# First chunk of tile 0's normalised rows: ScalarE writes the high part from the bank, VectorE the values beside it

## The chip, the core and the metric

The kernel runs on one core of one Trainium2 chip. The metric is the device time of one execution in microseconds (us). Three runs of the kernel before gave 1754.39, 1754.5 and 1756.76 us; their median is 1754.5 us.

The engines are named as the profile names them: PE (TensorE) multiplies, and its weight loads are PEld; DVE is VectorE, ACT ScalarE, POOL GpSimd; SP issues the loads from memory. Each works through its own list of instructions in order.

## The reference

One decoder layer on 256 rows of 2048 values in float32: a half-step SwiGLU FFN, then attention (eight MLA heads and eight NSA heads that read one combined input projection), then a second half-step FFN. After each of the three a DeepNorm layer norm:

```
x = layer_norm(ALPHA * x + 0.5 * swiglu(x, ffn1...), ln1_g, ln1_b)
mix = concat(mla(x @ w_in), nsa(x @ w_in)) @ w_out
x = layer_norm(ALPHA * x + mix, ln2_g, ln2_b)
x = layer_norm(ALPHA * x + 0.5 * swiglu(x, ffn2...), ln3_g, ln3_b)
```

## The kernel before

**Numbers in two parts.** PE reads operands in a rounded 32-bit format. To keep float32 accuracy each operand is held as a high part (the rounded value) and a low part (what the rounding left). `split` (L94 to L96) makes them: ACT casts the value to the high part, DVE subtracts the high part from the value. Weights become `whi` and `wlo`, activations `thi` and `tlo`. `mm3` (L98 to L102) makes one product of three matmuls, always in the order thi by whi (L100), thi by wlo (L101), tlo by whi (L102). PE takes them in that order, so the third one waits for `tlo` with all that follows.

**Stages.** FFN 1, input projection and attention, output projection, FFN 2. The 256 rows are two tiles of 128 rows (t = 0, 1). A row of 2048 values has four chunks of 512, n = 0 to 3. Weights stream from memory in pieces of 128 x 1024 (tiles `raw`, or `sum` from a second pool), which ACT and DVE split before PE uses them. So ACT and DVE serve two masters: the weight pieces, and everything that is done to activations.

**The layer norm in between.** When the last chunk of a tile's rows is complete, `ln` (L597) starts for that tile. DVE and ACT bring the rows to mean 0 and variance 1 (L594 to L608). Then `norm_T` (L567) goes chunk by chunk: PE turns the chunk's four 128 x 128 blocks round into one PSUM bank (L575). DVE takes blocks 0 and 2 out of the bank, multiplied by the gain and with the bias added (L584), ACT does the same for blocks 1 and 3 (L582), into a work tile `w`. At last `split` makes `thi` by an ACT cast of 128 x 512 (L95) and `tlo` by a DVE subtraction (L96). `w` is returned, since after the second layer norm sums of its blocks are needed too (L405 to L408).

`ln` runs this twice with consequences for the next stage: after FFN 1 (called ln1) for the input projection, and after attention (ln2) for FFN 2. In both, tile 0 goes first, while PE still finishes tile 1 of the stage before, and the next stage begins with products of chunk 0 of tile 0. Its first weight pieces are ready long before (they lie in tiles `m`).

**Who sets the order.** PE and SP take their instructions as the code issues them. ACT, DVE and POOL are put in order by a scheduler that plays the program through with times of its own, and gives the instruction of the highest priority that it holds ready; `tc.high_priority()` lifts what is written under it. Once built, the order is fixed. L384 and L1045 are DVE's additions of a finished bank to the residual rows `y` and L565 its statistics of them; they stand between the others in the lists below.

Of the kernel before, what the change touches and what calls it, by code (L numbers as in the profile page):

```python
# [13 lines left out]
AF = mybir.ActivationFunctionType  # L14
OP = mybir.AluOpType
# [38 lines left out]
def layer(ctx: ExitStack, tc: tile.TileContext, a: dict, out: bass.AP):  # L54
    nc = tc.nc
    PE, V, A, G = nc.tensor, nc.vector, nc.scalar, nc.gpsimd
# [12 lines left out]
    f = lambda t: t.bitcast(F32)  # L69
# [14 lines left out]
    def wk(shape):  # L84
        w = work.tile([P, NCH], F32, name="w", bufs=NW)
        if len(shape) == 3:
            return w[:, :shape[1] * shape[2]].rearrange("p (a b) -> p a b", a=shape[1])
        return w
# [5 lines left out]
    def split(hi, lo, src):  # L94
        A.copy(hi, src)  # L95
        V.tensor_tensor(lo, src, f(hi), op=OP.subtract)  # L96
# [87 lines left out]
    def new_bank():  # L184
        return bank.tile([P, NCH], F32, name="bank")
# [202 lines left out]
    def new_T():  # L388
        return (tp.tile([P, 4, P], F32R, name="thi"), tp.tile([P, 4, P], F32R, name="tlo"))
# [174 lines left out]
            st[t] = stat.tile([P, 4, 6], F32, name=f"bn{t}", bufs=1)  # L564
        V.bn_stats(st[t][:, n, :], y[t][:, n * NCH:(n + 1) * NCH])  # L565

    def norm_T(src, gcol, bcol, dst, k0):  # L567

        pt = new_bank().rearrange("p (a b) -> p a b", a=4)
        nj = src.shape[1] // P
        for j in range(nj):
            PE.transpose(pt[:, j, :], src[:, j * P:(j + 1) * P], ident)  # L575
        v = wk([P, 4, P])
        for j in range(nj):
            k = k0 + j
            if bcol is None:
                V.tensor_scalar(v[:, j, :], pt[:, j, :], gcol[:, k:k + 1], None, op0=OP.mult)  # L580
            elif j % 2:
                A.activation(v[:, j, :], pt[:, j, :], AF.Identity, bias=bcol[:, k:k + 1], scale=gcol[:, k:k + 1])  # L582
            else:
                V.tensor_scalar(v[:, j, :], pt[:, j, :], gcol[:, k:k + 1], bcol[:, k:k + 1], op0=OP.mult, op1=OP.add)  # L584
        if isinstance(dst, tuple):
            dst = [dst]
        step = nj // len(dst)
        for i, (hi, lo) in enumerate(dst):
            split(hi[:, :step, :], lo[:, :step, :], v[:, i * step:(i + 1) * step, :])
        return v  # L590

    def ln_rows(t, eps):
        mv = stat.tile([P, 2], F32, name="mv")
        V.bn_aggr(mv, st[t].rearrange("p a b -> p (a b)"))  # L594
        return mv[:, 0:1], rstd_of(mv[:, 1:2], eps)

    def ln(t, name, eps, x, xs=None):  # L597

        yc = [y[t][:, n * NCH:(n + 1) * NCH] for n in range(4)]
        with tc.high_priority():  # L600
            mu, r = ln_rows(t, eps)
            mr = stat.tile([P, 1], F32, name="mr")
            V.scalar_tensor_tensor(mr, mu, -1.0, r, op0=OP.mult, op1=OP.mult)
            for n in range(4):
                if n % 2 == 0:
                    V.tensor_scalar(yc[n], yc[n], mu, r, op0=OP.subtract, op1=OP.mult)
                else:
                    A.activation(yc[n], yc[n], AF.Identity, bias=mr, scale=r)  # L608
        yield DLN
        for n in range(4):  # L610
            x[n, t] = new_T()
            v = norm_T(yc[n], cst[name + "_g"], cst[name + "_b"], x[n, t], 4 * n)
            for j in range(2):
                if xs is not None and 2 * n + j in UP7:
                    xs.setdefault(2 * n + j, []).extend(v[:, 2 * j + i, :] for i in range(2))
            yield 1
# [20 lines left out]
    cst = {}  # L637
# [15 lines left out]
    def done1(t, n):  # L653
        ln_stats(t, n)
        if n == 3:
            spawn(ln(t, "ln1", 4 * LN_EPS, x1))
            steps()
# [49 lines left out]
    def fin_a(t, ps):  # L707
        def go():
            o = rms(ps, QR)
            yield DTR  # L710
            norm_T(o, cst["mla_q_norm_g"], None, lat(cq, t, 2), 0)

        spawn(go())
        steps()

    def fin_b(t, ps):
        def go():
            o = rms(ps[:, :KVR], KVR)
            kr = wk([P, 2, P])
            V.memset(kr, 0.0)  # L720
            rope(kr[:, 0:1, :RD], ps[:, KVR:KVR + RD].rearrange("p (h d) -> p h d", h=1), cst["cos64"][:, t, :],
                 cst["sin64"][:, t, :], 1, RD)
            V.tensor_copy(kr[:, 1, RD:], kr[:, 0, :RD])
            z = stat.tile([P, 24], F32, name="gz")
            V.tensor_tensor(z, ps[:, KVR + RD:KVR + RD + 24], cst["nsa_gate_b"], op=OP.add)
            A.activation(z, z, AF.Exp, scale=-1.0)
            V.tensor_scalar(z, z, 1.0, None, op0=OP.add)
            V.reciprocal(gates[:, t, :], z)
            yield DTR + 2
            norm_T(o, cst["mla_kv_norm_g"], None, lat(ckv, t, 1), 0)  # L730
            pt = new_bank().rearrange("p (a b) -> p a b", a=4)
            for j in range(2):
                PE.transpose(pt[:, j, :], kr[:, j, :], ident)
            A.copy(krT[:, :, t, :], pt[:, 0:2, :])

        spawn(go())
        steps()
# [315 lines left out]
    def out_last(ks, ns):  # L1053

        held = {}
        for t in range(NT):
            for n in ns:
                ps = new_bank()
                if t == 0:
                    held[n] = [(ks[i:i + KT], load(W["w_out"], n, ks[i:i + KT])) for i in range(0, len(ks), KT)]  # L1060
                for pc, wp in held[n]:
                    for k, (hi, lo) in zip(pc, wp):
                        mm3(ps, mixer(k, t), hi, lo, k == ks[0], k == ks[-1])
                    tick(1)
                out_fin(t, ps, n, False)
                ln_stats(t, n)
            spawn(ln(t, "ln2", LN_EPS, x2, xs2))
            steps()
# [123 lines left out]
```

## Time and profile before

| | |
|---|---|
| three runs | 1754.39, 1754.5, 1756.76 us, median 1754.5 us |
| the profiled execution | 1758.64 us, its span 1756.9 us |
| PE busy | 1736.7 us (99%) |
| DVE busy | 1586.5 us (90%) |
| ACT busy | 1023.5 us (58%) |
| granted TensorE clock, mean of the span | 0.997 |

The profile is of one execution, which took 4.1 us more than the median of the three runs; 1.7 us of its time lie outside the span. Times in a timeline are us from the start of the span. A row of it gives start, duration, engine, line, operation, what is written and read, how many instructions are merged in the row and, in square brackets, how long the engine had been idle and what ended that. Matmuls overlap, so what one of them costs is read from start to start (0.23 us for 128 x 512 at full clock), not from its duration; for ACT and DVE too the distance from start to start is a little shorter than the duration.

### The profile page before, as it was taken

What the parts mean: (1) busy time and instruction counts of PE and PEld (TensorE: products, weight loads), DVE (VectorE), ACT (ScalarE), POOL (GpSimd) and SP (SyncE); (2) the same over time, 40 slices, a digit from 0 to 9 for tenths busy, and PEclk for the clock granted to TensorE, in tenths of its full rate; (3) what the DMA queues carried; (4) which work ended last, traced back from release to release, by engine and by line L of the source; (5) the groups of instructions that cost most, each with busy time, mean ns of one, the idle gap of its engine ahead of it and who ended that gap; (6) DMA issues with size and microseconds to landing.
All of it is one profiled execution on the core that took longest, in us unless ns stands there. A gap on an engine that the chain in (4) does not pass through costs nothing. (4 is left out here: it accounts for less than half of the span.)

```text
span 1756.9 us, 22430 instructions
## 1 busy us (share of the span) xinstructions
PE 1736.7 (99%) x8040; PEld 1428.9 (81%) x8040; DVE 1586.5 (90%) x2099; ACT 1023.5 (58%) x1354; POOL 17.0 (1%) x39
## 2 busy tenths in 40 slices
PE   9999999999999999999999999999999999999997
PEld 7888888888888887887788788888888888888886
DVE  7899999999999998865586679899999999999998
ACT  6656565565656665654365545665655565656652
POOL 0000000000000000000000001000000000000000
PEclk9999999999999999999999999999999999999999
DMA  9665656556666566546753345654656655665665
GB/s 337 218 216 172 212 198 215 185 188 200 212 206 220 168 203 232 178 159 213 260 193 131 120 169 175 216 196 168 215 192 215 205 195 200 206 201 192 204 203 180
DMA packets 100336, 350.01 MB, mean 199 GB/s; under 512 B 11136, under 2 KB 13696, under 8 KB 100224
## 3 DMA queue, kind: packets, MB, share of 16 engines
q1 hardware_dynamic: 98944, 344.39, 58.4%
q0 software_dynamic: 1280, 4.20, 0.9%
q8 instruction: 63, 1.03, 0.2%
q14 instruction: 49, 0.40, 0.1%
HBM read 346.44 MB, written 2.10 MB: 198 GB/s over the span
## 5 line engine op out<-in xcount | busy, mean ns | idle before, releaser
L100 PE MATMUL bank<-whi,thi 128*128 128x512 f32 (+1 forms) x1904 | 748.6, 393 | 1.5 <-ACT whi L95 1.5
L101 PE MATMUL bank<-wlo,thi 128*128 128x512 f32 (+1 forms) x1904 | 740.8, 389 | 3.2 <-DVE wlo L96 3.1
L102 PE MATMUL bank<-whi,tlo 128*128 128x512 f32 (+1 forms) x1904 | 740.0, 389 | 0.2 <-DVE tlo L96 0.2
L95 ACT CAST whi<-raw 128x1024 fp32r<-128x1024 f32 (+1 forms) x577 | 540.6, 962 | 270.5 <-PE bank L102 142.9
L96 DVE TENSOR_TENSOR wlo<-raw,whi 128x1024 fp32r<-128x1024 f32 (+1 forms) x577 | 631.6, 1109 | 61.0 <-ACT whi L95 60.1
L95 ACT CAST whi<-sum 128x1024 fp32r<-128x1024 f32 x271 | 282.5, 1050 | 337.8 <-DVE sum L328 124.3
L100 PEld LDWEIGHTS bank<-whi,thi 128*128 128x128 f32 x1904 | 357.9, 188 | 79.3 <-issue 4.1
L101 PEld LDWEIGHTS bank<-wlo,thi 128*128 128x128 f32 x1904 | 358.1, 188 | 77.5 <-DVE wlo L96 7.0
L102 PEld LDWEIGHTS bank<-whi,tlo 128*128 128x128 f32 x1904 | 357.8, 188 | 74.3 <-DVE tlo L96 0.6
L96 DVE TENSOR_TENSOR wlo<-sum,whi 128x1024 fp32r<-128x1024 f32 x271 | 324.9, 1216 | 32.4 <-ACT whi L95 29.9
L100 PE MATMUL bank<-whi,m 128*128 128x512 f32 x448 | 174.3, 389 | 0.0
L101 PE MATMUL bank<-wlo,m 128*128 128x512 f32 x448 | 174.3, 389 | 0.0
L102 PE MATMUL bank<-whi,m 128*128 128x512 f32 x448 | 174.3, 389 | 0.0
L326 DVE TENSOR_TENSOR sum<-raw 128x1024 f32<-128x1024 f32 x112 | 136.7, 1220 | 12.4 <-DMA raw<-in_ffn_w_up 10.5
L101 PEld LDWEIGHTS bank<-wlo,m 128*128 128x128 f32 x448 | 84.1, 188 | 17.5
L102 PEld LDWEIGHTS bank<-whi,m 128*128 128x128 f32 x448 | 84.1, 188 | 17.5
L100 PEld LDWEIGHTS bank<-whi,m 128*128 128x128 f32 x448 | 84.1, 188 | 17.5
L328 DVE TENSOR_TENSOR sum<-sum,raw 128x512 f32<-128x512 f32 x112 | 76.9, 686 | 0.2
L327 DVE TENSOR_TENSOR sum<-sum,raw 128x512 f32<-128x512 f32 x112 | 76.8, 686 | 0.1
L384 DVE TENSOR_TENSOR w<-bank,w 128x512 f32<-128x512 f32 x80 | 51.8, 683 | 2.2 <-PE bank L102 2.2
L777 ACT ACTIVATE w<-w,mx 128x256 f32<-128x256 f32 (+1 forms) x48 | 21.3, 445 | 27.5 <-DVE mx L773 24.6
L384 DVE TENSOR_TENSOR y<-bank,w 128x512 f32<-128x512 f32 x32 | 20.7, 683 | 6.8 <-PE bank L102 6.8
(187 smaller groups left out, 946.5 us busy)
## 6 DMA issues: line engine op xcount, KB each, us to landing
raw<-in_ffn_w_down SPq DMA_DIRECT2D x176, 512.0 KB, 4.5
raw<-in_ffn_w_up SPq DMA_DIRECT2D x160, 512.0 KB, 4.7
raw<-in_ffn_w_gate SPq DMA_DIRECT2D x146, 512.0 KB, 4.7
raw<-in_ffn_gu SPq DMA_DIRECT2D x32, 512.0 KB, 5.0
raw<-in_w_in SPq DMA_DIRECT2D x30, 512.0 KB, 5.2
raw<-in_w_out SPq DMA_DIRECT2D x20, 512.0 KB, 3.3
sum<-in_w_in SPq DMA_DIRECT2D x18, 512.0 KB, 5.3
sum<-in_ffn_w_gate SPq DMA_DIRECT2D x12, 512.0 KB, 4.8
```

The costliest lines, as they stand in the source:

```text
L95: A.copy(hi, src)
L96: V.tensor_tensor(lo, src, f(hi), op=OP.subtract)
L100: PE.matmul(ps, xh, wh, start=first and not onto, stop=False, skip_group_check=onto)
L101: PE.matmul(ps, xh, wl, start=False, stop=False, skip_group_check=onto)
L102: PE.matmul(ps, xl, wh, start=False, stop=last, skip_group_check=onto)
L326: V.tensor_tensor(t13, a_, b_[:, 1:2, :].broadcast_to([P, 2, NCH]), op=OP.add)
L327: V.tensor_tensor(t24[:, 0], t13[:, 0], a_[:, 1], op=OP.add)
L328: V.tensor_tensor(t24[:, 1], t24[:, 0], b_[:, 0], op=OP.add)
L384: V.tensor_tensor(r, B[b], rest[b], op=OP.add)
L777: A.activation(s[:, h, :], s[:, h, :], AF.Exp, bias=mx[:, h:h + 1], accum_out=sm[:, h:h + 1])
```

## The change

`norm_T` gets a flag `first`, which `ln` sets for chunk 0 of tile 0 alone. It holds at both layer norms, so two of the sixteen chunks are concerned. For these, ACT writes all four blocks of `thi` straight from the bank, gain and bias applied (four instructions of 128 x 128), DVE writes the values of all four blocks into `w` beside it (four more), and DVE subtracts. The ACT cast of 128 x 512 is gone. All of it stands under `tc.high_priority()`.

```diff
-    def norm_T(src, gcol, bcol, dst, k0):
+    def norm_T(src, gcol, bcol, dst, k0, first=False):
...
         v = wk([P, 4, P])
+        if first:
+            with tc.high_priority():
+                for j in range(nj):
+                    g, b = gcol[:, k0 + j:k0 + j + 1], bcol[:, k0 + j:k0 + j + 1]
+                    A.activation(dst[0][:, j, :], pt[:, j, :], AF.Identity, bias=b, scale=g)
+                    V.tensor_scalar(v[:, j, :], pt[:, j, :], g, b, op0=OP.mult, op1=OP.add)
+                V.tensor_tensor(dst[1], v, f(dst[0]), op=OP.subtract)
+            return v
         for j in range(nj):
...
-            v = norm_T(yc[n], cst[name + "_g"], cst[name + "_b"], x[n, t], 4 * n)
+            v = norm_T(yc[n], cst[name + "_g"], cst[name + "_b"], x[n, t], 4 * n, t == 0 and n == 0)
```

In the changed kernel L581 is ACT's write of `thi`, L582 DVE's of `w`, L583 the subtraction; the lines that follow moved down by eight (DVE's L584 is L592, ACT's L582 is L590, L594 is L602, L1045 is L1053). PE, SP and POOL keep their orders. In the built program the eight instructions on the bank take turns: each L582 waits for the L581 of its block, and the next L581 for that L582.

DVE at ln1, from the first split of a weight piece after the rows were normalised to `tlo` of chunk 0 (the last row). Before, chunk 0's two and chunk 1's first two L584 and one of chunk 2 stand ahead of it:

```order
L96 TENSOR_TENSOR wlo<-raw,whi 128x1024
L584 TENSOR_SCALAR w<-bank,pack 128x128
L96 TENSOR_TENSOR wlo<-sum,whi 128x1024
L584 TENSOR_SCALAR w<-bank,pack 128x128 x2
L384 TENSOR_TENSOR y_93<-bank,w 128x512
L584 TENSOR_SCALAR w<-bank,pack 128x128
L565 BN_STATS bn_5629<-y_93 128x6
L584 TENSOR_SCALAR w<-bank,pack 128x128
L594 BN_AGGR mv<-bn_5629 128x2
L96 TENSOR_TENSOR tlo<-w,thi 128x512
```

Now, after the same `wlo<-raw`, another `wlo<-sum`, one L582 and one L592, the list goes on to `tlo` like this:

```order
L96 TENSOR_TENSOR wlo<-sum,whi 128x1024
L582 TENSOR_SCALAR w<-bank,pack 128x128
L592 TENSOR_SCALAR w<-bank,pack 128x128 x2
L582 TENSOR_SCALAR w<-bank,pack 128x128
L384 TENSOR_TENSOR y_93<-bank,w 128x512
L592 TENSOR_SCALAR w<-bank,pack 128x128
L565 BN_STATS bn_5629<-y_93 128x6
L582 TENSOR_SCALAR w<-bank,pack 128x128
L602 BN_AGGR mv<-bn_5629 128x2
L96 TENSOR_TENSOR wlo<-sum,whi 128x1024
L558 TENSOR_SCALAR rstd<-mv 128x1
L583 TENSOR_TENSOR tlo<-w,thi 128x512
```

Ahead of `tlo` of chunk 0 stand now three `wlo<-sum` instead of one, eight instructions of 128 x 128 instead of five, and `rstd` of tile 1.

ACT at the same place, from the first weight cast after the rows were normalised; before, up to the cast that makes `thi` of chunk 0:

```order
L95 CAST whi<-raw 128x1024
L95 CAST whi<-sum 128x1024 x2
L582 ACTIVATE w<-bank,pack 128x128
L95 CAST whi<-sum 128x1024
L95 CAST whi<-raw 128x1024
L582 ACTIVATE w<-bank,pack 128x128 x2
L95 CAST thi<-w 128x512
```

Now, up to the fourth block of chunk 0 (the cast of `thi` in it is chunk 1's):

```order
L95 CAST whi<-raw 128x1024
L95 CAST whi<-sum 128x1024
L581 ACTIVATE thi<-bank,pack 128x128
L95 CAST whi<-sum 128x1024 x2
L581 ACTIVATE thi<-bank,pack 128x128
L590 ACTIVATE w<-bank,pack 128x128
L95 CAST whi<-raw 128x1024
L581 ACTIVATE thi<-bank,pack 128x128
L590 ACTIVATE w<-bank,pack 128x128 x2
L95 CAST thi<-w 128x512
L581 ACTIVATE thi<-bank,pack 128x128
```

The first block comes earlier by one weight cast, but the fourth has the same five weight casts ahead of it, six small instructions instead of three, and chunk 1's cast.

DVE at ln2, from the last `wlo<-sum` before chunk 0 to `tlo` of chunk 0. Before:

```order
L96 TENSOR_TENSOR wlo<-sum,whi 128x1024
L584 TENSOR_SCALAR w<-bank,pack 128x128
L1045 TENSOR_TENSOR y_93<-bank,y_93 128x512
L584 TENSOR_SCALAR w<-bank,pack 128x128
L565 BN_STATS bn_9300<-y_93 128x6
L584 TENSOR_SCALAR w<-bank,pack 128x128
L96 TENSOR_TENSOR wlo<-raw,whi 128x1024
L96 TENSOR_TENSOR tlo<-w,thi 128x512
```

Now, after the same `wlo<-sum` and the addition to `y_93`:

```order
L582 TENSOR_SCALAR w<-bank,pack 128x128
L565 BN_STATS bn_9303<-y_93 128x6
L592 TENSOR_SCALAR w<-bank,pack 128x128
L96 TENSOR_TENSOR wlo<-raw,whi 128x1024
L582 TENSOR_SCALAR w<-bank,pack 128x128
L592 TENSOR_SCALAR w<-bank,pack 128x128 x2
L582 TENSOR_SCALAR w<-bank,pack 128x128
L1053 TENSOR_TENSOR y_93<-bank,y_93 128x512
L592 TENSOR_SCALAR w<-bank,pack 128x128
L582 TENSOR_SCALAR w<-bank,pack 128x128
L565 BN_STATS bn_9303<-y_93 128x6
L583 TENSOR_TENSOR tlo<-w,thi 128x512
```

Here `tlo` has eight instructions of 128 x 128 ahead of it instead of three, and one more addition to `y` with its statistics.

## The prediction

> **What bounds the kernel now.** I read the busy shares first, then the table of what PE waited for, then the timelines of PE, DVE and ACT round the two places of the change, and last the granted clock in stretches of 3.41 us.
>
> ```profile
> PE 1736.7 (99%) x8040; PEld 1428.9 (81%) x8040; DVE 1586.5 (90%) x2099; ACT 1023.5 (58%) x1354; POOL 17.0 (1%) x39
> PE bank L101 <- DVE wlo L96: 3.1, 6, 0.9
> PE bank L100 <- ACT thi L95: 2.2, 2, 1.8
> PE bank L100 <- ACT whi L95: 1.5, 3, 0.8
> PE bank L102 <- DVE tlo L96: 0.6, 2, 0.4
> ```
>
> PE has work for 99% of the span, so the end moves by what PE loses or gains. The rows on `thi` and `tlo` are the waits that the change can reach: 2.2 + 0.6 us in four waits. PE round ln1, and then ln2:
>
> ```profile
> 703.29 0.60 PE L575 MATMUL bank<-ident,y 128*128 128x128 f32 x4
> 705.64 0.50 PE L100 MATMUL bank<-m,thi 128*128 128x512 f32 x1 [1.75 <-ACT thi L95]
> 705.98 0.40 PE L101 MATMUL bank<-m,thi 128*128 128x512 f32 x1
> 706.37 0.50 PE L102 MATMUL bank<-m,tlo 128*128 128x512 f32 x1
> ...
> 709.01 0.40 PE L102 MATMUL bank<-m,tlo 128*128 128x512 f32 x1
> 709.32 0.51 PE L100 MATMUL bank<-whi,thi 128*128 128x512 f32 x1
> 709.66 0.39 PE L101 MATMUL bank<-wlo,thi 128*128 128x512 f32 x1
> 710.23 0.50 PE L102 MATMUL bank<-whi,tlo 128*128 128x512 f32 x1 [0.17 <-DVE tlo L96]
> 710.56 0.39 PE L100 MATMUL bank<-whi,thi 128*128 128x512 f32 x1
> ```
>
> ```profile
> 1051.24 0.60 PE L575 MATMUL bank<-ident,y 128*128 128x128 f32 x4
> 1052.33 0.50 PE L100 MATMUL bank<-m,thi 128*128 128x512 f32 x1 [0.50 <-ACT thi L95]
> 1052.67 0.40 PE L101 MATMUL bank<-m,thi 128*128 128x512 f32 x1
> 1053.48 0.50 PE L102 MATMUL bank<-m,tlo 128*128 128x512 f32 x1 [0.41 <-DVE tlo L96]
> ```
>
> Chunk 0 starts its two matmuls with `thi` (705.64, 705.98) and then needs `tlo` (706.37). Both `thi` and `tlo` are late, at ln1 by 1.75 us and a little, at ln2 by 0.50 and 0.41. Who makes them late is seen on DVE and ACT at ln1:
>
> ```profile
> 700.28 1.23 DVE L96 TENSOR_TENSOR wlo<-raw,whi 128x1024 fp32r<-128x1024 f32 x1 [0.38 <-ACT whi L95]
> 701.42 0.40 DVE L584 TENSOR_SCALAR w<-bank,pack 128x128 f32<-128x128 f32 x1
> 701.74 1.21 DVE L96 TENSOR_TENSOR wlo<-sum,whi 128x1024 fp32r<-128x1024 f32 x1
> 702.87 0.72 DVE L584 TENSOR_SCALAR w<-bank,pack 128x128 f32<-128x128 f32 x2
> 703.51 0.68 DVE L384 TENSOR_TENSOR y<-bank,w 128x512 f32<-128x512 f32 x1
> 704.11 0.40 DVE L584 TENSOR_SCALAR w<-bank,pack 128x128 f32<-128x128 f32 x1
> 704.43 0.68 DVE L565 BATCH_NORM_STATS2 bn<-y 128x6 f32<-128x512 f32 x1
> 705.12 0.41 DVE L584 TENSOR_SCALAR w<-bank,pack 128x128 f32<-128x128 f32 x1
> 705.44 0.25 DVE L594 BATCH_NORM_AGGREGATE mv<-bn 128x2 f32<-128x24 f32 x1
> 705.62 0.69 DVE L96 TENSOR_TENSOR tlo<-w,thi 128x512 fp32r<-128x512 f32 x1
> 706.23 0.15 DVE L558 TENSOR_SCALAR rstd<-mv 128x1 f32<-128x1 f32 x1
> 706.29 0.40 DVE L584 TENSOR_SCALAR w<-bank,pack 128x128 f32<-128x128 f32 x1
> ```
>
> ```profile
> 704.29 0.80 ACT L582 ACTIVATE w<-bank,pack 128x128 f32<-128x128 f32 x2
> 704.98 0.60 ACT L95 CAST thi<-w 128x512 fp32r<-128x512 f32 x1
> 705.49 0.81 ACT L582 ACTIVATE w<-bank,pack 128x128 f32<-128x128 f32 x2
> ```
>
> From 700.28 on DVE has no idle time until `tlo` is done, and ACT's rows follow each other too. Here neither engine waits for data: what counts is how much stands in the list ahead of `tlo`. PE's first matmul follows the end of the cast (704.98 + 0.60 = 705.58) by 0.06 us, its third the end of the subtraction (705.62 + 0.69 = 706.31) by 0.06 us.
>
> **The change part by part.** Each of the two chunks loses one ACT cast (0.60 us) and two L582, and gains four L581; DVE gains two instructions of 128 x 128. That work by itself is small and off the path on average (ACT is 58% busy). What counts is the order. The flag and the priority do put ACT's first block one weight cast earlier, so `thi` of block 0 is no longer what PE waits for. But `mm3` needs `tlo` as its third operand, and the one subtraction that makes it needs all four blocks.
>
> *tlo at ln1.* By the lists of DVE, up to `tlo` there are two more `wlo<-sum` (1.13 us each from start to start: 701.74 to 702.87), three more instructions of 128 x 128 (0.32 each: 701.42 to 701.74), and one `rstd` (0.06: 706.23 to 706.29). That is 2.26 + 0.96 + 0.06 = 3.28 us. ACT takes turns with DVE on the bank and holds it once: the third block has two more small ones ahead of it on ACT than the two L582 at 704.29 have (0.35 each: two of them take 704.29 to 704.98), so it ends at 704.29 + 0.70 + 0.45 = 705.44 (0.45 is one of two that take 0.80 together, 0.35 apart), while DVE would be there at 700.28 + 1.14 + 2 x 1.13 + 5 x 0.32 = 705.28. With 0.2 for this, `tlo` starts at 705.62 + 3.5 = 709.1, ends at 709.8, and the third matmul stands at 709.85 instead of 706.37: +3.5 us. ACT's fourth block is no later limit: 704.98 + 3 x 0.35 + 0.51 (the cast, 704.98 to 705.49) + 0.45 = 707.0.
>
> Some of it comes back. The four steps from 709.01 to 710.56 in the rows above take 1.55 us, of which the waits for chunk 1's parts and the restarts make 1.55 - 4 x 0.23 = 0.6. Chunk 1 is made sooner in the new lists, relative to PE, so these go. Net at ln1: +2.9 us.
>
> *tlo at ln2.* Here the list holds five more of 128 x 128 (5 x 0.32 = 1.6), one more addition to `y` (0.60, taken from 703.51 to 704.11) and its statistics (0.69, 704.43 to 705.12): 2.9 us, and with the same 0.2 for taking turns +3.1 us. PE's third matmul goes from 1053.48 to 1056.6. Behind it no wait is left to give back. Both waits hold everything behind them, since PE runs in order. SP's loads keep their order and come later by what PE is late, but so does their use.
>
> Together +6.0 us by waiting.
>
> *The clock.* The two waits are now single long ones: at ln1 from about 704.4 (transposes done at 703.89, then two matmuls) to 709.85, at ln2 from 1052.3 to 1056.6. What a gap does to the clock, in four stretches (columns: stretch, length, busy time of PE, PEld, DVE, ACT and POOL, clock, DMA, GB/s):
>
> ```profile
> 684.99:688.40 3.41, 1.73 (x6) 0.91 (x6) 1.81 (x4) 2.55 (x4) 0.00 (x0) 1.00 0.76 274
> 688.40:691.81 3.41, 3.41 (x10) 2.63 (x9) 3.08 (x6) 0.78 (x2) 0.00 (x0) 0.50 0.98 362
> 702.05:705.46 3.41, 1.84 (x11) 1.29 (x9) 3.40 (x8) 3.41 (x7) 0.00 (x0) 1.00 0.62 159
> 705.46:708.88 3.42, 3.24 (x15) 2.40 (x16) 3.07 (x9) 3.42 (x7) 0.55 (x1) 1.00 0.13 48
> ```
>
> A stretch in which PE was busy 1.73 of 3.41 us was followed by one at clock 0.50; one with 1.84 us was not. With the change 705.46 to 708.88 holds no matmul at all, so the next stretch, to 712.29, runs at half clock: PE works in it from 709.85, and loses half of 2.4, 1.2 us. At ln2, shifted by 2.9 + 1.2, the gap lies from 1056.4 to 1060.7; in steps of 3.41 the stretch 1057.04 to 1060.45 is empty, and half clock lasts to 1063.87: half of 3.2, 1.6 us. Together +2.8 us. How the gap lies to the stretches is chance in another run; moving it through one stretch, I estimate 0.9 to 2.4 us for each.
>
> The Trainium skill ("TensorE: Matmul & The Clock Gate", Part 1: The HAM clock gate) has the clock halved after an idle window of about 3.4 us, and windows that run freely. This trace is stricter: 688.40 followed a stretch that was half busy. By the page's rule a whole window must be idle, which a gap of 5.4 us need not hold and one of 4.3 seldom does; by it the clock would cost 0 to 2.8 us, and the sum would be 6.0 to 8.8.
>
> *Sum.* 6.0 + 2.8 = +8.8 us: the profiled execution's 1758.64 would be 1767.4, and the median of 1754.5, which is 4.1 lower, 1763.3 us.
>
> **The rivals.** *The priority works on the chip* (the other side). If DVE came to `tlo` no later than PE needs it, the losses at both places would go: at ln1 1.75, then 0.16 (705.98 to 706.37, less 0.23), then 0.6; at ln2 0.50 and 0.58 (1052.67 to 1053.48, less 0.23): 3.6 us, 1750.9. It decides where 3.3 us of DVE's list would vanish at ln1; DVE has no idle time there before, and the list is fixed. Chance 0.03.
>
> *Half of the shift only.* DVE's extra entries are the same weight pieces that it split right behind `tlo` before. If PE could use the work done early, a part of the wait would be paid back. Then +3, 1757.5. Against it: after 710.56 only few waits remain on PE to shorten. Chance 0.05.
>
> *No half clock, or at one place alone.* Waiting as forecast, 6.0 to 7.2 us: 1760.5 to 1761.7. For it: a stretch with 1.84 us of work kept the full clock after it. Against it: the gaps are longer than one stretch. Chance 0.2. The page's rule above is of this kind, its milder end.
>
> *Half clock for a stretch longer at each place*, if the stretch in which PE restarts doesn't count as busy: up to 1.7 us more each, half of 3.41: 1765 to 1766.7. For it: the one case in the trace was released only after a stretch with PE busy throughout (3.41). Chance 0.12.
>
> **How the numbers follow.** The forecast, waits and half clock at both places, has 0.6: 1763.3, with 1762 to 1765 as its own range. About 0.2%, 3.5 us, is what a measurement of this kernel can tell from no change. Faster by more than that (below 1751.0) is only the first rival at its full price: 0.02. Within it lie the rest of that rival and the half shift: 0.06. Slower: 0.92. The range leaves out the first two rivals (0.08) and what lies above a longer half clock: 1759.5 to 1767.0, which takes in the lowest case without half clock less 1 us for the two sums of waits.
>
> **What would show it.** In the profile of the changed kernel PE's row L102 at about 709.8 and at about 1060.7 should show the wait for `tlo` from L583, 5 and 4 us long, and L100 none for `thi`; the subtraction L583 should start near 709.1, on a DVE without idle time since 700.28 but for 0.2; the stretches behind the two gaps should have clock 0.50. Wrong would be: L583 done before 706.4, or the wait there but PE caught up by 720, or no stretch at 0.50 beside the one at 688.

## The result and the profile after

The changed kernel took 1766.09 us (median of 4 runs, 1765.72 to 1766.55) beside 1755.55 us (1754.39 to 1756.76, 4 runs: the three above and one of 1756.59) of the kernel before: ratio 1.0057, 95% interval 1.0045 to 1.0069. It is slower by 0.6%. The time lies inside the predicted range of 1759.5 to 1767.0, but 2.8 us above the predicted 1763.3 and 1.1 above the forecast's own 1762 to 1765; 1.05 of the 2.8 us are the fourth run's share in the median of before. Its profiled execution took 1765.87 us, with a span of 1764.2 us.

What PE waited for at `thi` and `tlo` is one row now (us in total, times, longest us); the row on `thi` is gone:

```profile
PE bank L102 <- DVE tlo L583: 9.6, 2, 5.3
```

PE at ln1, with the two matmuls that no longer wait and the third that does:

```profile
700.82 0.48 PE L100 MATMUL bank<-m,thi 128*128 128x512 f32 x1
701.14 0.40 PE L101 MATMUL bank<-m,thi 128*128 128x512 f32 x1
706.84 0.79 PE L102 MATMUL bank<-m,tlo 128*128 128x512 f32 x1 [5.31 <-DVE tlo L583]
707.43 0.63 PE L100 MATMUL bank<-m,thi 128*128 128x512 f32 x1
707.86 0.63 PE L101 MATMUL bank<-m,thi 128*128 128x512 f32 x1
...
710.84 0.40 PE L100 MATMUL bank<-m,thi 128*128 128x512 f32 x1
711.09 0.40 PE L101 MATMUL bank<-m,thi 128*128 128x512 f32 x1
...
712.01 0.40 PE L102 MATMUL bank<-whi,tlo 128*128 128x512 f32 x1
```

The two matmuls with `thi` run as soon as the transposes are done. The third waits 5.31 us, and the matmuls behind it come 0.43 us apart instead of 0.23, until 710.84. DVE meanwhile, from the same first weight piece as before:

```profile
697.45 1.22 DVE L96 TENSOR_TENSOR wlo<-raw,whi 128x1024 fp32r<-128x1024 f32 x1 [0.38 <-ACT whi L95]
698.60 1.22 DVE L96 TENSOR_TENSOR wlo<-sum,whi 128x1024 fp32r<-128x1024 f32 x1
699.73 0.40 DVE L582 TENSOR_SCALAR w<-bank,pack 128x128 f32<-128x128 f32 x1
...
704.49 0.40 DVE L582 TENSOR_SCALAR w<-bank,pack 128x128 f32<-128x128 f32 x1
704.80 0.25 DVE L602 BATCH_NORM_AGGREGATE mv<-bn 128x2 f32<-128x24 f32 x1
704.97 1.16 DVE L96 TENSOR_TENSOR wlo<-sum,whi 128x1024 fp32r<-128x1024 f32 x1
706.04 0.14 DVE L558 TENSOR_SCALAR rstd<-mv 128x1 f32<-128x1 f32 x1
706.10 0.68 DVE L583 TENSOR_TENSOR tlo<-w,thi 128x512 fp32r<-128x512 f32 x1
```

From the first weight piece to the start of `tlo` it is now 706.10 - 697.45 = 8.65 us; before it was 705.62 - 700.28 = 5.34. ACT's four blocks were ready before; the last one ended at 704.17, 1.93 us ahead of `tlo`:

```profile
703.69 0.48 ACT L581 ACTIVATE thi<-bank,pack 128x128 fp32r<-128x128 f32 x1
```

At ln2 the same picture, with a wait of 4.25 us:

```profile
1053.27 0.48 PE L100 MATMUL bank<-m,thi 128*128 128x512 f32 x1
1053.58 0.40 PE L101 MATMUL bank<-m,thi 128*128 128x512 f32 x1
1058.23 0.50 PE L102 MATMUL bank<-m,tlo 128*128 128x512 f32 x1 [4.25 <-DVE tlo L583]
...
1062.44 0.40 PE L102 MATMUL bank<-m,tlo 128*128 128x512 f32 x1
```

Taking turns shows there as a wait of DVE, once:

```profile
1056.58 0.41 DVE L582 TENSOR_SCALAR w<-bank,pack 128x128 f32<-128x128 f32 x1 [0.21 <-ACT thi L581]
```

The clock in stretches of 3.41 us, at ln1 (three) and at ln2 (three):

```profile
700.60:704.02 3.42, 0.93 (x7) 0.50 (x5) 3.32 (x8) 3.42 (x9) 0.00 (x0) 1.00 0.82 224
704.02:707.43 3.41, 0.59 (x1) 0.50 (x2) 2.97 (x8) 2.07 (x5) 0.93 (x1) 0.50 0.17 59
707.43:710.85 3.42, 3.42 (x12) 2.73 (x11) 3.42 (x6) 1.52 (x2) 0.00 (x0) 0.50 0.37 103
```

```profile
1052.18:1055.59 3.41, 1.80 (x10) 1.15 (x9) 3.41 (x8) 3.14 (x8) 0.00 (x0) 1.00 0.55 185
1055.59:1059.01 3.42, 0.78 (x3) 0.67 (x4) 3.21 (x9) 1.92 (x5) 0.00 (x0) 1.00 0.40 129
1059.01:1062.42 3.41, 3.41 (x11) 2.73 (x10) 2.97 (x6) 1.52 (x2) 0.86 (x1) 0.50 0.00 0
```

PE's order is the same in both kernels, so each matmul of the one can be set beside the same matmul of the other. Its start after less its start before shows where time was lost (the times of before at 691.57 and later are those of its profiled execution):

| the same instruction of PE | before | after | after less before |
|---|---|---|---|
| a matmul of the last product of FFN 1 | 691.57 | 688.88 | -2.69 |
| first matmul with `thi`, ln1 | 705.64 | 700.82 | -4.82 |
| first matmul with `tlo`, ln1 | 706.37 | 706.84 | +0.47 |
| a matmul at the end of the half clock | 708.55 | 710.84 | +2.29 |
| third matmul of the first product with chunk 1 | 710.23 | 712.01 | +1.78 |
| first matmul with `tlo`, ln2 | 1053.48 | 1058.23 | +4.75 |
| a matmul at the end of the half clock | 1056.11 | 1062.44 | +6.33 |
| last matmul | | | +7.2 |

From 691.57 to the end the changed kernel lost 7.2 + 2.7 = 9.9 us: at ln1 3.16 by the wait and 1.8 by the clock, of which 0.5 came back; at ln2 2.97 and 1.6; the remaining 0.9 came between 1466 and 1480 us (times of before). The 2.7 us ahead of that are a loss of the kernel before in its one profiled execution; `priority_alone` below takes them up.

### The profile page after: what moved, and what is told of

Same layout as the page of the kernel before. It is cut to its first block, busy times and chain, and to the rows that moved or that the text cites. A ratio compares the mean times of both kernels' runs of the same rounds, so it can differ in the third digit from the quotient of the medians.

```text
span 1764.2 us, 22435 instructions
## 1 busy us (share of the span) xinstructions
PE 1738.3 (99%) x8040; PEld 1431.3 (81%) x8040; DVE 1588.2 (90%) x2103; ACT 1024.3 (58%) x1356; POOL 17.7 (1%) x39
## 5 line engine op out<-in xcount | busy, mean ns | idle before, releaser
L516 DVE TENSOR_TENSOR w<-w 128x512 f32<-128x512 f32 x40 | 25.6, 679 | 0.0
```

The costliest lines, as they stand in the source:

```text
L516: V.tensor_tensor(hs[c0 + j, t], r, sg[c0 + j, t], op=OP.mult)
```

## The experiments

**Each place by itself.** The changed kernel, with the flag at one layer norm only:

```diff
-..., 4 * n, t == 0 and n == 0)
+..., 4 * n, t == 0 and n == 0 and name == "ln1")
```

and `"ln2"` in the second.

> The change at ln1 alone; ln2 as in the kernel before. Theory (the wait for tlo and the half clock behind it are paid at each place by itself): in the profile of the changed kernel PE's lag behind the kernel before grows by 4.5 us across ln1 (from -2.7 at 691.6 us to +1.8 at 710.2) and by 4.6 across ln2, so about 1755.6 + 4.5 = 1760.1 us, with one wait for L583 of 5.3 us and one stretch or two at clock 0.50 behind it. Rival (the second place waits only because the first one shifted everything): nearly the whole loss stays with ln1, 1764 us or more.

> The change at ln2 alone; ln1 as in the kernel before. Theory (each place pays by itself): 1755.6 + 4.6 = 1760.2 us, with one wait for L583 of 4.3 us. Rival (ln2 waits only because ln1 shifted everything): no more than 1756.5 us.

Measured: `ln1_only` 1760.89 us (ratio to the kernel before 1.0027, interval 1.0016 to 1.0038), `ln2_only` 1760.95 us (1.0026, 1.0016 to 1.0036). PE's row on L583 in the two, `ln1_only` first:

```profile
PE bank L102 <- DVE tlo L583: 5.3, 1, 5.3
```

```profile
PE bank L102 <- DVE tlo L583: 4.3, 1, 4.3
```

Each place pays half, with the wait it has in the changed kernel. The rival that the one causes the other is out.

**What the clock costs.** The changed kernel with PE kept at work through the wait. `fill` is 22 at the input projection and 17 at FFN 2:

```diff
+    fill = []
+
     def mm3(ps, x, wh, wl, first, last, onto=False):
         xh, xl = x
+        for _ in range(fill.pop() if fill else 0):
+            PE.matmul(ps, xh, wh, start=True, stop=True)
         PE.matmul(ps, xh, wh, start=first and not onto, stop=False, skip_group_check=onto)
...
+    fill.append(22)
...
+    fill.append(17)
```

> The changed kernel, but PE repeats the first matmul of the input projection 22 times and the first one of FFN 2 17 times (each repetition begins its bank anew, so nothing of the result changes), which fills about 5.0 and 3.9 us of the waits for tlo. DVE's and ACT's lists up to tlo stay. Theory (the gap halves the clock, and that costs 1.8 us behind ln1 and 1.6 behind ln2, as PE's rows show): the third matmuls come at the same times, no stretch of 0.50 follows, and the time is 1766.1 - 3.4 = 1762.7 us. Rival (the matmuls behind the wait are slow for another reason than the gap, as operands that come late): still 1766 us, with matmuls 0.43 us apart behind the wait.

Measured: 1763.05 us (ratio 1.0039, 1.0024 to 1.0054), 3.0 us less than the changed kernel, though PE does 39 matmuls more. PE at ln1:

```profile
700.20 5.28 PE L103 MATMUL bank<-m,thi 128*128 128x512 f32 x22
...
705.55 0.39 PE L105 MATMUL bank<-m,thi 128*128 128x512 f32 x1
706.23 0.50 PE L106 MATMUL bank<-m,tlo 128*128 128x512 f32 x1 [0.29 <-DVE tlo L587]
...
706.79 0.40 PE L105 MATMUL bank<-m,thi 128*128 128x512 f32 x1
707.02 0.40 PE L106 MATMUL bank<-m,tlo 128*128 128x512 f32 x1
```

The third matmul starts 706.23 - 700.20 = 6.03 us behind the first one with `thi`, in the changed kernel 706.84 - 700.82 = 6.02, and the matmuls that follow come 0.23 us apart again. No stretch at 0.50 is left between PE's first matmuls and its last. So the half clock behind the gaps cost about 3 us of the 10.5; operands that come late behind the wait are out as its cause.

**Taking turns.** The same eight instructions, named by the code in another order:

```diff
                 for j in range(nj):
                     g, b = gcol[:, k0 + j:k0 + j + 1], bcol[:, k0 + j:k0 + j + 1]
                     A.activation(dst[0][:, j, :], pt[:, j, :], AF.Identity, bias=b, scale=g)
+                for j in range(nj):
+                    g, b = gcol[:, k0 + j:k0 + j + 1], bcol[:, k0 + j:k0 + j + 1]
                     V.tensor_scalar(v[:, j, :], pt[:, j, :], g, b, op0=OP.mult, op1=OP.add)
```

> The same eight instructions on the bank at both places, but written as ACT's four first and then DVE's four, so that ACT and DVE take turns once instead of seven times. Theory (taking turns makes the scheduler believe that tlo comes late, and lets weight pieces in ahead of it; the instructions themselves cost next to nothing): L583's counterpart now has at ln1 two splits of weight pieces and five small ones ahead of it instead of four and eight; PE's wait for it is then an estimated 0.7 us at ln1 and 1.7 at ln2, no clock of 0.50 behind them, and the time 1755.2 us (1754 to 1757). Rival (the two more small instructions of each engine, and two readers on one bank, are the cost): the same instructions stay, so 1764 to 1766 us.

Measured: 1755.86 us (ratio 0.9999, 0.999 to 1.0009). DVE and then PE at ln1:

```profile
697.65 1.22 DVE L96 TENSOR_TENSOR wlo<-sum,whi 128x1024 fp32r<-128x1024 f32 x1
698.86 1.37 DVE L584 TENSOR_SCALAR w<-bank,pack 128x128 f32<-128x128 f32 x4
700.14 0.41 DVE L594 TENSOR_SCALAR w<-bank,pack 128x128 f32<-128x128 f32 x1
700.46 0.69 DVE L585 TENSOR_TENSOR tlo<-w,thi 128x512 fp32r<-128x512 f32 x1
```

```profile
700.19 0.40 PE L101 MATMUL bank<-m,thi 128*128 128x512 f32 x1
701.20 0.50 PE L102 MATMUL bank<-m,tlo 128*128 128x512 f32 x1 [0.62 <-DVE tlo L585]
```

With one hand-over between ACT and DVE instead of seven, the scheduler puts DVE's four in a row and `tlo` behind them, with one small instruction of chunk 1 (L594) between. PE waits 0.62 us at ln1 (1.49 at ln2), and the whole loss is gone, to within the interval of 0.1%, with not one instruction less. The added work is not the cost.

**A bank each.** To tell whether the shared bank makes them take turns, or the code's order: the change at ln1 alone, with PE turning the chunk round a second time into another bank:

```diff
+            p2 = new_bank().rearrange("p (a b) -> p a b", a=4)
+            for j in range(nj):
+                PE.transpose(p2[:, j, :], src[:, j * P:(j + 1) * P], ident)
...
-                    V.tensor_scalar(v[:, j, :], pt[:, j, :], g, b, op0=OP.mult, op1=OP.add)
+                    V.tensor_scalar(v[:, j, :], p2[:, j, :], g, b, op0=OP.mult, op1=OP.add)
```

> The change at ln1 alone (as in ln1_only, 1760.9 us), but PE turns chunk 0 round twice, into two banks: ACT reads the one, DVE the other, in the code's order of the change. Theory (it is the shared bank that makes the two take turns, and the turns put tlo late in DVE's list): with a bank each no turns are left, tlo comes in the list right behind five small instructions, PE's wait for it goes, no clock of 0.50 follows, and PE gains an estimated 1.5 us on the kernel before, in spite of four more transposes: 1754.4 us (1753 to 1756). Rival (the order in which the code names the instructions sets it, not the bank): 1760.9 us, as in ln1_only.

Measured: 1754.79 us (ratio 0.9994, 0.9985 to 1.0003), 6 us less than `ln1_only` with the same order in the code. DVE and PE at ln1:

```profile
695.72 1.23 DVE L96 TENSOR_TENSOR wlo<-raw,whi 128x1024 fp32r<-128x1024 f32 x1 [0.39 <-ACT whi L95]
696.87 1.36 DVE L585 TENSOR_SCALAR w<-bank,pack 128x128 f32<-128x128 f32 x4
698.15 0.40 DVE L595 TENSOR_SCALAR w<-bank,pack 128x128 f32<-128x128 f32 x1
698.47 0.68 DVE L586 TENSOR_TENSOR tlo<-w,thi 128x512 fp32r<-128x512 f32 x1
```

```profile
699.54 0.48 PE L100 MATMUL bank<-m,thi 128*128 128x512 f32 x1
699.86 0.39 PE L101 MATMUL bank<-m,thi 128*128 128x512 f32 x1
700.09 0.40 PE L102 MATMUL bank<-m,tlo 128*128 128x512 f32 x1
```

`tlo` is done at 699.15, and PE passes all three matmuls without a wait. So at ln1 it is the shared bank that makes them take turns, and the code's order alone does not; at ln2 a bank each was not tried. The Trainium skill ("PSUM — Partial Sum Buffer", on bank collisions) says why a program must keep the two apart: reads of one bank by ACT and DVE at the same time, on the same group of 32 partitions, raise an error on trn2, even at different columns. No run here lets them collide. Against the kernel before, `two_banks_ln1` is not told apart by its interval, though its median is the lowest measured here.

**One subtraction for four blocks.** The changed kernel, with the subtraction inside the loop:

```diff
-                V.tensor_tensor(dst[1], v, f(dst[0]), op=OP.subtract)
+                    V.tensor_tensor(dst[1][:, j, :], v[:, j, :], f(dst[0])[:, j, :], op=OP.subtract)
```

> The changed kernel at both places, but tlo is subtracted block by block, four times 128 x 128, each behind its own block. Theory (PE's third matmul waits since the one subtraction needs all four blocks): the one long wait falls apart into shorter ones, an estimated 0.8, 1.0 and 2.4 us at ln1 and 1.1 at ln2 with 2.3 before a transpose there, each too short for an empty stretch of 3.41 us, so that the half clock mostly goes: 1755.9 + 1.6 + 2.1 = 1759.6 us. Rival (the long wait is DVE's work on weight pieces, however tlo is cut): 1765 to 1767 us, with waits of 4 to 5 us.

Measured: 1758.03 us (ratio 1.0011, 1.0002 to 1.002). PE's waits at ln1:

```profile
701.56 0.50 PE L102 MATMUL bank<-m,tlo 128*128 128x512 f32 x1 [0.46 <-DVE tlo L583]
703.72 0.50 PE L102 MATMUL bank<-m,tlo 128*128 128x512 f32 x1 [0.50 <-DVE tlo L583]
706.43 0.50 PE L102 MATMUL bank<-m,tlo 128*128 128x512 f32 x1 [1.66 <-DVE tlo L583]
```

In place of one wait of 5.3 us there are three, 2.6 us together, with matmuls between them and no half clock; block 0's matmul does not wait. So in the changed kernel PE was held by blocks 1 to 3 for an operand of block 0. At ln2 a wait of 0.59 us for `tlo` is left, and one of 1.81 ahead of a transpose. The estimate was 1.6 us too high, each wait being shorter than estimated. This kernel is still 0.1% slower than the one before.

**Priority alone.** The operations of the kernel before under `tc.high_priority()`:

```diff
+        with tc.high_priority() if first else ExitStack():
             for j in range(nj):
...
```

> The operations of the kernel before, with the first chunk's under high priority. The lists of all engines come out as in the kernel before, so this is also a second profile of those lists. Theory (the priority does nothing here, neither good nor harm): 1755.9 us as before, with waits for thi and tlo of 1.8 and 0.5 us as before; and the 2.7 us that the profiled execution of before lost between 685 and 692 us are chance of that one execution, so they are not here. Rival (the priority carries the loss): 1760 us or more. For the 2.7 us: if the lists themselves cause them, a stretch of 0.50 stands near 688 again.

Measured: 1755.68 us (ratio 1.0, 0.9991 to 1.0009). DVE, ACT, POOL and PE run the same instructions in the same order as in the kernel before: with those operations the priority moves nothing. The changed kernel without the priority was not run. Near 688 no half clock appears, and the same matmul that stood at 691.57 stands at 688.37. So the 2.7 us are chance of the one execution of before. But another stretch is halved, at ln1:

```profile
699.92:703.34 3.42, 1.67 (x8) 0.95 (x7) 3.42 (x10) 3.42 (x8) 0.22 (x1) 1.00 0.63 186
703.34:706.75 3.41, 3.41 (x11) 2.73 (x10) 3.06 (x7) 3.40 (x7) 0.34 (x1) 0.50 0.00 0
```

## Why the prediction was right, and where it was off

- *The list, not the data, sets when `tlo` comes.* Right. It priced the longer list at 3.28 us and 0.2 for taking turns, 3.5 together; DVE came to `tlo` 8.65 - 5.34 = 3.31 us later and PE's third matmul lost 3.16 at ln1. At ln2 it priced 3.1 and PE lost 2.97. The 0.6 us that come back were 0.5.
- *What taking turns costs.* The 0.2 us as a direct wait were right at ln2 (0.21 us, where L582 waits for L581); at ln1 the 3.31 us leave next to nothing for it. But the prediction did not see that taking turns is also why the list is as it is. `acts_first` and `two_banks_ln1` show it: without the turns the same operations, under the same priority, go ahead of the weight pieces, and the loss is gone. That the scheduler sees `tlo` come late when the eight must alternate, and fills in what it holds ready, is argued from these lists and not shown, since its own times were not looked at.
- *Half clock.* Right in kind, 1.6 us at ln2 as forecast. At ln1 the term of 1.2 us was too small: measured 1.8. The stretches lay otherwise than in the execution before. The halving began at 704.02, in the middle of the wait, and lasted two stretches; in the first of them PE was busy for 0.59 us only, and it worked from 706.84 to 710.85 at half speed. So the rival with a stretch more at each place came true at ln1 and not at ln2, and the measured 1766.1 us lie in that rival's 1765 to 1766.7, which had the chance 0.12. How the gap lies to the stretches was named as chance; that the term at ln2 came out to 0.1 us is luck in this sense, since the stretch forecast there as empty (1057.04 to 1060.45) was not: the halving followed a stretch with 0.78 us of work.
- *The milder rule*, that a whole window must be idle, is not borne out: no stretch of the changed kernel at ln1 or ln2 was empty of work (0.93, 0.59, 0.78 us), and still the clock was halved at both, at a cost of 3.4 us in the trace and 3.0 in `pe_busy`, beside 0 to 2.8 by that rule. In `ln1_only` and `ln2_only` the halved clock did follow an empty stretch, so these two traces fit either rule. The two other ways out fell as well: priority that works (under it `tlo` came 3.31 us later; alone, in `priority_alone`, it changes nothing) and a shift that is half paid back (PE's lag stays at about +1.7 from 712 until ln2).
- *The sum.* Predicted +8.8; PE's rows give +9.9 and the medians +10.5. From 8.8 to 9.9 the clock at ln1 adds 0.6, a little less given back 0.1 and the loss between 1466 and 1480 us, which no step foresaw, 0.9, while the two waits, priced a little too high, take off 0.5. The other 0.6 lie between two profiled executions and the medians of four runs. In that loss PE waits once for a weight's low part (a row of the changed kernel, at its own later time):

```profile
1486.67 0.50 PE L101 MATMUL bank<-wlo,thi 128*128 128x512 f32 x1 [0.50 <-DVE wlo L96]
```

  `priority_alone` loses 0.6 us against the kernel before at the same matmul with the lists of before, so at least this part is chance. The rest stays open.

## What to carry to other kernels

A new pair of readers on one PSUM bank can become a chain of hand-overs, and a scheduler that counts the chain may put the end of it behind everything else that is ready; group the reads by engine, or give each its own bank, before reaching for priorities. Read the built order up to the operand that PE needs last, here `tlo`: moving its partner `thi` ahead gained nothing. And price a wait on PE with the half clock behind it; here it cost 3.4 us beside the 6.1 us that PE lost by the two waits themselves.

## What the runs showed of the hardware

In the middle of the kernel a stretch of 3.41 us at full clock was followed by half clock when PE had been busy in it for 0.78, 0.93, 1.67 or 1.73 us, and not when it had been busy for 1.80 or 1.84 us (six stretches, of the kernel before, the changed kernel and `priority_alone`). So a wait of 1.75 us can halve the clock or not, by how it falls into the stretches: the kernel before's lists had both at ln1, 1.84 us of work with full clock behind it and 1.67 us with half (`priority_alone`). The Trainium skill ("TensorE: Matmul & The Clock Gate", Part 1) speaks of an idle window; these traces differ from that, and the measurement decides.

But the busy time alone does not fix the step. Behind PE's last matmuls the full clock went on although PE had been busy for 1.67 us (the changed kernel, first two rows) and 1.72 us (`pe_busy`, third row):

```profile
1751.91:1755.33 3.42, 1.67 (x8) 1.05 (x6) 3.32 (x6) 0.00 (x0) 0.00 (x0) 1.00 0.41 153
1755.33:1758.74 3.41, 0.00 (x0) 0.00 (x0) 3.37 (x7) 0.00 (x0) 0.92 (x1) 1.00 0.03 11
1747.91:1751.33 3.42, 1.72 (x8) 1.10 (x6) 3.35 (x6) 0.00 (x0) 0.00 (x0) 1.00 0.41 153
```

There the matmuls follow each other without a gap, while in the halved stretches waits lie between or behind them, and a matmul that stands alone counts as busy for 0.5 us (686.67 and 687.93 in the kernel before: 0.49 and 0.50). Counted from start to start, 0.23 us for a matmul of 128 x 512 and 0.35 for four transposes (700.47 to 700.82 in the changed kernel), the four halved stretches hold 0.7 to 1.1 us of work and the four others 1.5 to 1.6. This is an estimate from the rows of these stretches; where between the two the step lies is not shown.

A stretch at half clock was followed by another when PE was busy in it for 0.59 us (the changed kernel) or 2.00 us (`ln1_only`, the row below), and by full clock when PE had been busy for 2.82 us (`ln2_only`) or throughout.

```profile
705.88:709.29 3.41, 2.00 (x5) 1.51 (x6) 2.97 (x8) 2.06 (x4) 0.93 (x1) 0.50 0.34 96
```
